# A two-layer fp32 decoder trunk: a seventh-product block more per column group, and weight sums written by adding DMAs

## The chip, the cores and the metric

The kernel runs on one core of a Trainium2 chip, as one launch. The metric is the device time of that launch in microseconds (us). TensorE (PE) multiplies, VectorE (DVE) and ScalarE (ACT) work elementwise, GpSimd (POOL) does small operations, and SyncE (SP) issues the DMAs. In this program POOL's queue can issue DMAs as well.

## The reference

x has 256 tokens of 2048 features; there are two layers, all in fp32. Cut to what matters:

```python
for i in range(2):
    sh1, sc1, g1, sh2, sc2, g2 = split(silu(c) @ w_mod[i] + b_mod[i], 6)
    h = rms_norm(x, norm1_g[i]) * (1 + sc1) + sh1
    y = retention_mixer(h) if i == 0 else short_conv_mixer(h)
    x = x + g1 * y
    h = rms_norm(x, norm2_g[i]) * (1 + sc2) + sh2
    a, b = split(h @ ffn_w_in[i], 2)          # 2048 x 11264
    x = x + g2 * ((silu(a) * b) @ ffn_w_out[i])   # 5632 x 2048
return rms_norm(x, final_g)
```

The feed-forward part (SwiGLU) of each layer multiplies by `ffn_w_in` (first matrix) and `ffn_w_out` (second matrix). They are most of the work.

## The kernel before

**Stages.** The profile shows them one after the other: retention (to about 790 us), the feed-forward of layer 0 ("FFN", to about 1480), the convolution layer (to about 1860) and the feed-forward of layer 1 (the "last stage").

**fp32 by three products.** Every weight tile is split into a rounded part `hi` (ACT, L415) and a remainder `lo` (DVE, L418: raw minus hi); activations are split in the same way. A product is then hi·hi + hi·lo + lo·hi: three matmuls (`thrice`, L481 to L483).

**Weights.** The host lays all weights out in order of use in `w_all`, in chunks of 128 x 2048. SP loads a chunk into one of four buffers `raw` (L376). `prepare` makes pieces of up to 128 x 1024 from it: `hi`, `lo`, and an entry in `ready`. `hi` and `lo` hold five such places, so preparation runs at most five pieces ahead of PE. The same `raw` buffers also take the columns of `w_mod`, each reduced against silu(c) by one DVE instruction over 2048 columns (L322, a "modulation"); there are 160 of these, and `paced` hands them out by a table of due times, `plan_mod`, in units of 128x128 weight tiles used.

**Column groups.** The first matrix of a feed-forward is done in 10 groups after some first columns. A group covers four tiles of `a` and four of `b` (two blocks of 512 columns) and runs through eight pairs of rows ("rows 0 to 7"), each one chunk. It accumulates over the rows in four PSUM banks (`ours`, 128 tokens x 512 each). There are eight banks in all.

**Sevens.** A row given in `IN_SEVEN`, `FFN_SEVEN` or `OUT_SEVEN` is a `Seven`: its 2 x 2 blocks of tokens, rows and columns are multiplied in seven products instead of eight (Strassen's scheme in Winograd's form). That is 7 x 3 matmuls of 512 columns instead of 8 x 3. For the activations, sums of blocks are made once per stage (`made_in_sums`). For the weights, four sums are made per chunk: T1 and T3 in one DVE instruction of 1024 columns (L402, into the tile `differences`), T2 (L406) and T4 (L408) in one of 512 each. The sevens' four extra sums (`p1`, `p5`, `p6`, `p7`) build up in four further banks, and after the group's last seven `mixed_sums` takes them out: one ACT copy (L1202) and four DVE instructions (L1203 to L1206). The next group's `ours` use these banks. After the last row, DVE adds `ours` (L1258), then silu and product follow (L1262, L1263). At row 2 of the next group (`TURNS_AT`, `FFN_TURNS`), PE transposes the result into two banks (`turned`, L1272), and ACT (L1276) and DVE (L1277) split it. The sevens of the next group need those two banks for p1 and p6.

**Order.** Only PE's order (and DVE's and ACT's at the very start) is written by hand. On the other engines a scheduler places the instructions; modulations get a low priority.

Of the kernel before, what the change touches and what calls it, by code (L numbers as in the profile page):

```python
# [260 lines left out]
def trunk(ctx: ExitStack, tc: tile.TileContext, x_in, c_in, pos_in, w_mod, cols_in, gain_in, tab_in, w_all, out):  # L261
# [40 lines left out]
    nc.vector.memset(half, -0.5)  # L302

    flat = [v.rearrange("p a b -> p (a b)") for v in x4]
    differences = [None]


    mod_a = [[const.tile([P, KT], F32, tag=f"a{l}{i}", name=f"a{l}{i}") for i in range(2)] for l in range(DEPTH)]
# [80 lines left out]
    def prepare(between=None):  # L389
        if prepared[0] == len(pieces):  # L390
            return
        index, piece = pieces[prepared[0]]
        prepared[0] += 1
        if piece in (0, 2, 6):
            raws[:] = [next_raw(index)]
            while first <= units[0] < early and len(fetched) < RAW_BUFS - 1 and n_fetched[0] < w_all.shape[0]:
                fetch()
        whole = raws[0]
        b = [whole[:, i : i + DV] for i in range(0, CHUNK, DV)]
        raw = whole[:, :HALF] if piece in (0, 4) else whole[:, HALF:] if piece < 6 else whole  # L400
        if piece == 2:
            nc.vector.tensor_tensor(differences[0], whole[:, DV : 3 * DV], whole[:, : 2 * DV], op=ALU.subtract)  # L402
        elif piece == 3:
            raw = differences[0]
        elif piece == 4:
            nc.vector.tensor_tensor(b[1], b[2], differences[0][:, :DV], op=ALU.subtract)  # L406
        elif piece == 5:
            nc.vector.tensor_tensor(b[3], b[3], b[1], op=ALU.subtract)  # L408
            raw = b[3]
        width, at = raw.shape[1], HALF * (taken_places[0] % PLACES)  # L410
        taken_places[0] += -(-width // HALF)
        hi, lo = [t[:, at : at + width] for t in split_weights]
        steps = [slice(i, min(i + HALF, width)) for i in range(0, width, HALF)]
        for o in steps:
            nc.scalar.copy(hi[:, o], raw[:, o])  # L415
        if between:
            between()
        nc.vector.tensor_tensor(lo, raw, hi.bitcast(F32), op=ALU.subtract)  # L418
        ready.extend((hi[:, o], lo[:, o], o.stop - o.start) for o in steps)

    taken_places = [0]
    split_weights = [
        wpool.tile([P, PLACES * HALF], F32R, tag=tag, name=tag) for tag in ("hi", "lo")
# [34 lines left out]
    def product(g, act, base=0, before=None, banks=None, last=True):  # L458

        fresh = not banks  # L460
        banks = banks or [bank() for _ in g.cols]
        for k in g.ks:
            if before:
                before(k)
            h = act[k - base]
            for c, pt in zip(g.cols, banks):
                hi, lo = take(g, k, c)
                nc.tensor.matmul(  # L468
                    pt, hi, h, start=fresh and k == g.ks[0], stop=False, skip_group_check=True
                )  # L470
                nc.tensor.matmul(  # L471
                    pt[:, 1, :], lo, h[:, 0, :], start=False, stop=last and k == g.ks[-1], skip_group_check=True
                )
            ticked(len(g.cols))
        paced(len(g.cols) * len(g.ks))
        return banks

    def thrice(o, x, w, first, last):
# [14 lines left out]
    def packed(g, act, base=0, before=None, between=None, banks=None, plain=()):  # L493
# [5 lines left out]
        for k in g.ks:  # L499
# [32 lines left out]
                nc.tensor.matmul(pt, lo, h[:, 0, :], start=False, stop=last, skip_group_check=True)  # L532
                at += 1
            ticked(g.n)
        paced(g.n * len(g.ks))
        return banks

    def summed(pt, dst=None, at=slice(0, S)):
# [11 lines left out]

    def squares(acc, t, tag="acc"):
        if acc is None:
            acc = tmp(tag, bufs=1)
            nc.scalar.activation(acc, t, AF.Square)
        else:
            sq = tmp("sq", bufs=2)
# [83 lines left out]
    def normed(accs, layer, norm, g):  # L640
# [18 lines left out]
        for k in g.ks:  # L659
            high, low = raw_all[:, k, : ENDS + S], raw_all[:, k, ENDS + S :]  # L660
            for c, pt in zip(g.cols, banks):
                hi, lo = take(g, k, c)
                nc.tensor.matmul(pt, hi, high, start=k == 0, stop=False, skip_group_check=True)  # L663
                nc.tensor.matmul(pt[:, 2:], hi, low, start=False, stop=False, skip_group_check=True)  # L664
                nc.tensor.matmul(pt, lo, high, start=False, stop=k == KT - 1, skip_group_check=True)  # L665
            if k == ROOTS_AT:
                r = norm_roots(norm_sums(accs), D)
            elif k == SPREAD_AT:
                root = tmp("rb", bufs=1)
                nc.scalar.copy(root, norm_spread(r))  # L670
            elif k > SPREAD_AT:
                more(min(k, made[0] + 2))
        more(KT)
        paced(len(g.cols) * len(g.ks))

        def total(pt, dst=None):
            low_end = tmp("end", (P, 1), bufs=4)
# [478 lines left out]
    def tokens_sums_of(a11, a21, a12, a22, third, others):  # L1156

        u = half_bank()
        s1, s2, s4, s3 = [u[:, n * P : (n + 1) * P] for n in range(4)]
        nc.vector.tensor_tensor(s3, a11, a21, op=ALU.subtract)  # L1160
        nc.vector.tensor_tensor(s1, a21, a22, op=ALU.add)
        nc.vector.tensor_tensor(s2, s1, a11, op=ALU.subtract)
        nc.vector.tensor_tensor(s4, a12, s2, op=ALU.subtract)
# [33 lines left out]
    def mixed_sums(banks):  # L1197

        p1, p5, p6, p7 = banks
        u1, u3 = own["extra"]  # L1200
        u2, u4 = half_bank(), half_bank()
        nc.scalar.copy(u1, p1)  # L1202
        nc.vector.tensor_tensor(u2, p6, u1, op=ALU.add)  # L1203
        nc.vector.tensor_tensor(u3, p7, u2, op=ALU.add)
        nc.vector.tensor_tensor(u4, p5, u3, op=ALU.add)
        nc.vector.tensor_tensor(u2, p5, u2, op=ALU.add)  # L1206
        return {(0, 0): u1, (1, 0): u3, (1, 1): u4, (0, 1): u2}


# [73 lines left out]
    def first_rows(firsts, pairs, layer, norm, turns=()):  # L1283

        pending, done = [], 0
        for i, g in enumerate(firsts):
            pending += [sums(g)] if i else normed(acc, layer, norm, g)
            while len(pending) >= 2:
                both = half_bank().rearrange("p (a b) -> p a b", a=2)
                g1, m = both[:, 0, :], both[:, 1, :]  # L1290
                silu_times(*pending[:2], g1, m)
                pending = pending[2:]
                split(pairs[done // 2][:, done % 2], m)
                done += 1
            for turn_of in turns[4 * (i - 1) : 4 * i] if i else ():
                turn_of()

    def paired(pool, n):
# [3 lines left out]
    with tc.tile_pool(name="ffn", bufs=1) as fpool:  # L1302
        h = rows_at(EARLIER)
        own.update(pool=fpool, sums={}, turns=FFN_TURNS)
        first_mid = paired(fpool, max(FFN_TILES))[: FFN_TILES[0] // 2]
        differences[0] = fpool.tile([P, 2 * DV], F32, tag="differences", name="differences")
        own["extra"] = [fpool.tile([P, DV], F32, tag=f"extra{i}", name=f"extra{i}") for i in range(2)]
        for part in range(2):
            n = FFN_TILES[part] // 2
            mid = paired(fpool, FFN_TILES[part]) if part else first_mid  # L1310
            if not part:
                first_rows(FFN_FIRSTS, mid[-2:], 0, 1)
                made_in_sums(FFN_SEVEN, [
                    fpool.tile([P, 2, P], F32R, tag=f"sums{i}", name=f"sums{i}") for i in range(3 * len(FFN_SEVEN))
                ])
# [48 lines left out]
    differences[0] = flat[2]  # L1364
    xt = [mpool.tile([P, D], F32, tag=f"xt{t}", name=f"xt{t}") for t in range(2)]

    def turn(t, c):
# [15 lines left out]
    def three(v):  # L1383
        return [v[0][:, :, n * P : (n + 1) * P] for n in range(3)] if len(v) == 1 else v

    turns = [lambda t=t, c=c: turn(t, c) for c in range(4) for t in range(2)]


    gate_of = [at(flat[c // 2], c % 2) for c in range(4)]
# [91 lines left out]
    for part in range(2):  # L1481
        n = LAST_TILES[part] // 2
        mid = mids(LAST_TILES[part]) if part else first_mid
        if not part:
            first_rows(LAST_FIRSTS, mid[-2:], 1, 1, turns)
            tmp("beside_sums", (P, BESIDE_SUMS), bufs=1)
            for tag, bufs in (("u", 3), ("low", 2), ("sum", 4)):
# [46 lines left out]
```

## Time and profile before

| what | value |
|---|---|
| median of 3 runs | 2574.0 us (2573.86 to 2575.99) |
| the profiled execution's own time | 2574.43 us |
| its span in the profile | 2572.7 us |
| PE / DVE / ACT / POOL busy | 99% / 89% / 51% / 8% |
| DMA queue of SP, share of 16 engines | 71.5% |
| mean granted TensorE clock | 0.998 |

The span is what the profile shows of the execution; 1.7 us of its own time lie around it. A busy PE is not PE at its peak: its matmuls overlap, so work on PE is counted below by the distance from one start to the next.

### The profile page before, as it was taken

The numbers are of one execution on the slowest core, as the hardware profiler recorded it, in microseconds if no ns is written. First come the engines' busy times: TensorE is split into PE (matmuls) and PEld (weight loads), VectorE is DVE, ScalarE is ACT, GpSimd is POOL, SyncE is SP. The second block draws the span as 40 slices with busy tenths as digits, with TensorE's granted clock in tenths as the row PEclk, the third lists the DMA queues.
The fourth block names the chain that finished last, engine by engine and source line by source line (L and its number), as shares of the span: only waits on it lengthen the run. The fifth ranks groups of instructions, "written<-read, shape, count | busy, mean of one in ns | idle before, by whom it ended". The sixth has DMA issues, their size and how long they took to land.

```text
span 2572.7 us, 35163 instructions
## 1 busy us (share of the span) xinstructions
PE 2553.4 (99%) x13561; PEld 2202.8 (86%) x13561; DVE 2287.4 (89%) x2840; ACT 1312.1 (51%) x1723; POOL 198.8 (8%) x232
## 2 busy tenths in 40 slices
PE   8999999999999999999999999999999999999998
PEld 6898889888889888888888898888998888888887
DVE  7988978888699999888999989988989998899987
ACT  5544543444456554345555454444565554555554
POOL 0000102211000111100001112000000000000002
PEclk9999999999999999999999999999999999999999
DMA  9986769877786777876767869887945565555653
GB/s 399 389 330 234 298 247 351 305 264 296 263 305 235 284 279 289 326 285 249 268 246 288 320 248 351 314 325 271 332 167 214 179 235 206 178 215 183 227 196 131
DMA packets 96697, 689.51 MB, mean 268 GB/s; under 512 B 10744, under 2 KB 12168, under 8 KB 13456
## 3 DMA queue, kind: packets, MB, share of 16 engines
q1 hardware_dynamic: 96528, 687.25, 71.5%
q8 instruction: 106, 1.74, 0.3%
q14 instruction: 63, 0.52, 0.1%
HBM read 685.11 MB, written 2.11 MB: 267 GB/s over the span
## 4 chain that ended last, share of the span: by engine, by line
PE 94%; DVE 3%; DMA 2%; issue 1%; ACT 1%; SPq 0%; ACTq 0%; POOLq 0%; POOL 0%; DVEq 0%
PE bank L481 18%; PE bank L483 18%; PE bank L482 18%; PE bank L468 18%; PE bank L471 10%; PE bank L532 2%; PE bank L531 2%; PE bank L530 2%; PE bank L663 1%; PE bank L665 1%; PE bank L664 1%; DVE lo L418 1%; DMA raw<-w_all 1%; DVE raw L794 1%; PE bank L1272 1%
## 5 line engine op out<-in xcount | busy, mean ns | idle before, releaser
L415 ACT CAST hi<-raw 128x1024 fp32r<-128x1024 f32 (+1 forms) x968 | 983.6, 1025 | 1019.0 <-PE bank L483 459.0
L418 DVE TENSOR_TENSOR lo<-raw,hi 128x1024 fp32r<-128x1024 f32 (+1 forms) x968 | 1134.9, 1185 | 210.6 <-ACT hi L415 204.6
L481 PE MATMUL bank<-hi,h 128*128 128x512 f32 x1580 | 618.3, 391 | 0.0
L483 PE MATMUL bank<-hi,h 128*128 128x512 f32 x1580 | 615.9, 390 | 0.0
L482 PE MATMUL bank<-lo,h 128*128 128x512 f32 x1580 | 615.9, 390 | 0.0
L322 DVE SCALAR_TENSOR_TENSOR raw<-raw,cb 128x2048 f32<-128x2048 f32 x160 | 365.2, 2283 | 8.8 <-DMA raw<-w_mod 8.5
L483 PEld LDWEIGHTS bank<-hi,h 128*128 128x128 f32 x1580 | 296.6, 188 | 62.9
L481 PEld LDWEIGHTS bank<-hi,h 128*128 128x128 f32 x1580 | 296.9, 188 | 59.4
L482 PEld LDWEIGHTS bank<-lo,h 128*128 128x128 f32 x1580 | 296.9, 188 | 59.2 <-DVE lo L418 0.4
L468 PE MATMUL bank<-mid,hi 128*128 128x512 f32 x920 | 319.4, 390 | 0.0
L471 PE MATMUL bank<-mid,lo 128*128 128x256 f32 x920 | 259.4, 282 | 0.0
L468 PE MATMUL bank<-h,hi 128*128 128x512 f32 x736 | 255.4, 390 | 0.0
L471 PE MATMUL bank<-h,lo 128*128 128x256 f32 x736 | 207.4, 282 | 0.0
L468 PEld LDWEIGHTS bank<-mid,hi 128*128 128x128 f32 x920 | 172.6, 188 | 36.2
L471 PEld LDWEIGHTS bank<-mid,lo 128*128 128x128 f32 x920 | 173.9, 189 | 0.1
L468 PE MATMUL bank<-rm,hi 128*128 128x512 f32 x496 | 172.6, 391 | 0.0
L468 PEld LDWEIGHTS bank<-h,hi 128*128 128x128 f32 x736 | 138.1, 188 | 28.9
L532 PE MATMUL bank<-h,lo 128*128 128x256 f32 x488 | 138.5, 284 | 2.6 <-DVE lo L418 2.6
L471 PE MATMUL bank<-rm,lo 128*128 128x256 f32 x496 | 140.1, 282 | 0.2 <-DVE lo L418 0.2
L530 PE MATMUL bank<-h,hi 128*128 128x256 f32 x488 | 138.4, 284 | 1.3 <-ACT h L822 1.3
L471 PEld LDWEIGHTS bank<-h,lo 128*128 128x128 f32 x736 | 139.1, 189 | 0.0
L531 PE MATMUL bank<-h,hi 128*128 128x256 f32 x488 | 138.1, 283 | 0.1
(281 smaller groups left out, 3513.0 us busy)
## 6 DMA issues: line engine op xcount, KB each, us to landing
raw<-w_all SPq DMA_DIRECT2D x456, 1024.0 KB, 4.9
raw<-w_mod SPq DMA_DIRECT2D x192, 1024.0 KB, 5.6
x<-x_in SPq DMA_DIRECT2D x4, 512.0 KB, 5.4
out<-xt SPq DMA_DIRECT2D x4, 512.0 KB, 3.0
decay<-tab_in SPq DMA_DIRECT2D x8, 128.0 KB, 4.7
x<-gate_row SPq DMA_DIRECT2D x2, 512.0 KB, 4.4
last_gain<-gain_in SPq DMA_DIRECT2D x1, 1024.0 KB
cols<-cols_in SPq DMA_DIRECT2D x1, 152.0 KB, 8.1
```

Source lines behind the costliest of these rows:

```text
L322: nc.vector.scalar_tensor_tensor(raw, raw, 1.0, cb, op0=ALU.mult, op1=ALU.mult, accum_out=total)
L415: nc.scalar.copy(hi[:, o], raw[:, o])
L418: nc.vector.tensor_tensor(lo, raw, hi.bitcast(F32), op=ALU.subtract)
L468: nc.tensor.matmul(pt, hi, h, start=fresh and k == g.ks[0], stop=False, skip_group_check=True)
L471: nc.tensor.matmul(pt[:, 1, :], lo, h[:, 0, :], start=False, stop=last and k == g.ks[-1], skip_group_check=True)
L481: nc.tensor.matmul(o, hi, w_hi, start=first, stop=False)
L482: nc.tensor.matmul(o, hi, w_lo, start=False, stop=False)
L483: nc.tensor.matmul(o, lo, w_hi, start=False, stop=last)
L530: nc.tensor.matmul(pt, hi, h[:, 0, :], start=first, stop=False, skip_group_check=True)
L531: nc.tensor.matmul(pt, hi, h[:, 1, :], start=False, stop=False, skip_group_check=True)
L532: nc.tensor.matmul(pt, lo, h[:, 0, :], start=False, stop=last, skip_group_check=True)
L663: nc.tensor.matmul(pt, hi, high, start=k == 0, stop=False, skip_group_check=True)
```

## The change

It makes these edits:

1. `IN_SEVEN` goes from three rows to four of eight (2, 3, 5, 6), and `FFN_SEVEN` from two (3, 5) to three (2, 4, 6).
2. In the last stage T1 and T3 of a seven are no longer made by DVE. SP loads columns 512 to 1535 of the chunk a second time into a sum tile (`sum_begun`), and two prepared pieces later a DMA issued by POOL adds columns 0 to 1023 to it as it writes (`sums_added`). Four sum tiles take turns: the tile `squares_of`, the two halves of a `raw` buffer that is kept from the ring (so three are left for the chunks), and `flat[2]`.
3. All weight sums are now additions; the signs move to the sums of the activations and to `mixed_sums`. In layer 0 DVE still makes T1 and T3.
4. `plan_mod` hands out more modulations in retention and fewer in the FFN, and `paced` is called once per row instead of once per group.
5. Tiles of the norm move into `squares_of`, the order of the transposes of x changes, and the scratch for DMA descriptors is doubled.

```diff
-IN_SEVEN, OUT_SEVEN, TURNS_AT, BESIDE_CB, BESIDE_SUMS = (3, 4, 6), ((2, 4, 6), (2, 4, 6)), 2, 40, 48
+IN_SEVEN, OUT_SEVEN, TURNS_AT, BESIDE_CB, BESIDE_SUMS = (2, 3, 5, 6), ((2, 4, 6), (2, 4, 6)), 2, 40, 48
-FFN_TILES, FFN_SEVEN, FFN_TURNS = (20, 24), (3, 5), 2
+FFN_TILES, FFN_SEVEN, FFN_TURNS = (20, 24), (2, 4, 6), 2
+ADD_AFTER = 2
...
-    plan_mod = [(early, 0), (1024, 22), (1984, 58), (2688, 74), (3008, 88), (3776, 104), (5184, n_mod)]
+    plan_mod = [(early, 0), (1024, 28), (1984, 72), (2688, 84), (3008, 96), (3776, 106), (5184, n_mod)]
...
-        allowed[0] = min(allowed[0] + n * MOST, 2.0) if n <= 64 else 0.0
+        allowed[0] = min(allowed[0] + n * MOST, 2.0)
...
-        if piece == 2:
-            nc.vector.tensor_tensor(differences[0], whole[:, DV : 3 * DV], whole[:, : 2 * DV], op=ALU.subtract)
+        if piece == 2 and index not in summing:
+            summing[index] = sum_tiles[0]
+            nc.vector.tensor_tensor(summing[index], whole[:, DV : 3 * DV], whole[:, : 2 * DV], op=ALU.add)
         elif piece == 3:
-            raw = differences[0]
+            raw = summing[index]
         elif piece == 4:
-            nc.vector.tensor_tensor(b[1], b[2], differences[0][:, :DV], op=ALU.subtract)
+            nc.vector.tensor_tensor(b[1], b[0], summing.pop(index)[:, DV:], op=ALU.add)
         elif piece == 5:
-            nc.vector.tensor_tensor(b[3], b[3], b[1], op=ALU.subtract)
+            nc.vector.tensor_tensor(b[3], b[3], b[1], op=ALU.add)
...
+        if piece == 4:
+            sum_begun()
+        sums_added(1)
+
+    def sum_begun():
+        if len(sums_due) > sums_end[0]:
+            index = sums_due.pop(0)
+            sum_tiles.append(sum_tiles.pop(0))
+            summing[index] = sum_tiles[-1]
+            nc.sync.dma_start(summing[index], w_all[index, :, DV : 3 * DV])
+            adding.append([index, ADD_AFTER])
+
+    def sums_added(n):
+        for a in adding:
+            a[1] -= n
+        while adding and adding[0][1] <= 0:
+            index = adding.pop(0)[0]
+            nc.gpsimd.dma_start(summing[index], w_all[index, :, : 2 * DV], accum_op=ALU.add)
+
+    def sums_from(tiles, end, n):
+        sum_tiles[:], sums_end[0] = tiles, end
+        for _ in range(n):
+            sum_begun()
...
+            if turns and i < 2:
+                tiles = [flat[2], *sum_tiles] if i else [squares_of, *more_sums()]
+                sums_from(tiles, 0, 1 if i else len(tiles))
...
+    def more_sums():
+        held_raw = wpool.tile([P, CHUNK], F32, tag="raw", name=name("raw"), bufs=RAW_BUFS)
+        return [held_raw[:, i : i + 2 * DV] for i in range(0, 4 * DV, 2 * DV)]
```

Three places where the instructions stand differently:

**DVE, end of a column group in the FFN.** `u` and `extra` are the tiles of `mixed_sums` and of the group's end, `lo` the remainders of the weights. Before, from `mixed_sums` (L1203) to the adds of `ours` (L1258):

```order
L1203 TENSOR_TENSOR u_1162_10040<-bank_9936,extra_6782 128x512
L418 TENSOR_TENSOR lo<-raw_10047,hi 128x1024
L1204 TENSOR_TENSOR extra_6783<-bank_9937,u_1162_10040 128x512
L418 TENSOR_TENSOR lo<-raw_10047,hi 128x1024
L1205 TENSOR_TENSOR u_1163_10041<-bank_9935,extra_6783 128x512
L1206 TENSOR_TENSOR u_1162_10040<-bank_9935,u_1162_10040 128x512
L418 TENSOR_TENSOR lo<-raw_10082,hi 128x1024 x2
L1258 TENSOR_TENSOR extra_6782<-bank_9820,extra_6782 128x512
```

With the change the same instructions are L1232 to L1235, L421 and L1287:

```order
L1232 TENSOR_TENSOR u_1166_10133<-bank_9965,extra_6855 128x512
L421 TENSOR_TENSOR lo<-raw_10118,hi 128x1024
L1233 TENSOR_TENSOR extra_6856<-bank_9966,u_1166_10133 128x512
L421 TENSOR_TENSOR lo<-raw_10140,hi 128x1024
L1234 TENSOR_TENSOR u_1167_10134<-bank_9964,extra_6856 128x512
L1235 TENSOR_TENSOR u_1166_10133<-bank_9964,u_1166_10133 128x512
L421 TENSOR_TENSOR lo<-raw_10140,hi 128x1024
L1287 TENSOR_TENSOR extra_6855<-bank_9879,extra_6855 128x512
```

The group's last seven is row 6 instead of row 5, so `mixed_sums` stands one row later: one `lo` lies between it and the adds, where two lay.

**PE, row 2 of a column group in the FFN.** The last of the eight transposes and what follows. Before, row 2 is an ordinary row and goes into the four banks of `ours`:

```order
L1272 MATMUL bank_8067<-tab,extra_6783 128x128
L481 MATMUL bank_7995<-hi,h 128x512
L482 MATMUL bank_7995<-lo,h 128x512
L483 MATMUL bank_7995<-hi,h 128x512
L481 MATMUL bank_7997<-hi,h 128x512
L482 MATMUL bank_7997<-lo,h 128x512
```

With the change it is a seven (`u` are sums of activations):

```order
L1301 MATMUL bank_8163<-tab,extra_6856 128x128
L508 MATMUL bank_8085<-hi,u_7441 128x512
L509 MATMUL bank_8085<-lo,u_7441 128x512
L510 MATMUL bank_8085<-hi,u_7441 128x512
L508 MATMUL bank_8084<-hi,h 128x512
L509 MATMUL bank_8084<-lo,h 128x512
L510 MATMUL bank_8084<-hi,h 128x512
L508 MATMUL bank_8171<-hi,u_7443 128x512
```

The seven begins right behind the transposes; its fifth product (p1) needs the first of the two banks that the transposes just wrote, its sixth (p6) the second. In the last stage rows 2 and 3 stand in the same way.

**SP, steady part of the last stage.** Loads of chunks (`raw` from `w_all`, 128x2048). Before, there is nothing else in its queue:

```order
L376 DMA raw_2085_18993<-w_all 128x2048
L376 DMA raw_2086_19011<-w_all 128x2048
L376 DMA raw_2089_19033<-w_all 128x2048
L376 DMA raw_2094_19075<-w_all 128x2048
L376 DMA raw_2095_19105<-w_all 128x2048
```

With the change (128x1024 are the first halves of the sums):

```order
L378 DMA raw_2065_19293<-w_all 128x2048
L432 DMA raw_1836_16436<-w_all 128x1024
L378 DMA raw_2066_19311<-w_all 128x2048
L432 DMA x8_75<-w_all 128x1024
L378 DMA raw_2067_19358<-w_all 128x2048
L378 DMA raw_2068_19393<-w_all 128x2048
L432 DMA squares_81<-w_all 128x1024
L378 DMA raw_2069_19411<-w_all 128x2048
L432 DMA raw_1836_16436<-w_all 128x1024
L378 DMA raw_2072_19433<-w_all 128x2048
```

Of eight chunks of a group four are followed by a load into a sum tile (`squares`, the two halves of raw_1836, `x8`, which is `flat[2]`). Each waits until DVE has read its tile for the last time (T2 of a seven whose chunk stands two loads further up), and fills it for the seven four further on.

More of the change, by code (lines that the diff above doesn't have):

```diff
@@ L304, in trunk @@
     flat = [v.rearrange("p a b -> p (a b)") for v in x4]
-    differences = [None]
+    squares_of = const.tile([P, 4 * S], F32, tag="squares", name="squares")
+    n_squares = [0]
     mod_a = [[const.tile([P, KT], F32, tag=f"a{l}{i}", name=f"a{l}{i}") for i in range(2)] for l in range(DEPTH)]
@@ L419, in prepare @@
         ready.extend((hi[:, o], lo[:, o], o.stop - o.start) for o in steps)
+        if piece == 4:
[18 more added lines that the diff above has]
+            sum_begun()
+    summing, sums_due, sum_tiles, sums_end, adding = {}, [], [], [0], []
     taken_places = [0]
@@ L474, in product @@
             ticked(len(g.cols))
-        paced(len(g.cols) * len(g.ks))
+            paced(len(g.cols))
         return banks
@@ L672, in normed @@
                 more(min(k, made[0] + 2))
+            paced(len(g.cols))
         more(KT)
-        paced(len(g.cols) * len(g.ks))
         def total(pt, dst=None):
@@ L1305, in trunk @@
         first_mid = paired(fpool, max(FFN_TILES))[: FFN_TILES[0] // 2]
-        differences[0] = fpool.tile([P, 2 * DV], F32, tag="differences", name="differences")
+        sum_tiles[:] = [fpool.tile([P, 2 * DV], F32, tag="weights", name="weights")]
+        last_sevens = sum(isinstance(g, Seven) for part in range(2) for g in sum(LAST_IN[part] + LAST_OUT[part], []))
+        sums_due[:], sums_end[0] = sorted(in_seven)[-last_sevens:], last_sevens
         own["extra"] = [fpool.tile([P, DV], F32, tag=f"extra{i}", name=f"extra{i}") for i in range(2)]
@@ L1313, in trunk @@
                 made_in_sums(FFN_SEVEN, [
-                    fpool.tile([P, 2, P], F32R, tag=f"sums{i}", name=f"sums{i}") for i in range(3 * len(FFN_SEVEN))
-                ])
+                    fpool.tile([P, 2, P], F32R, tag=f"sums{i}", name=f"sums{i}") for i in range(6)
+                ] + [tmp("u", (P, 2, P), F32R, bufs=3) for _ in range(3)])
             for i, groups in enumerate(FFN_IN[part]):
@@ L1384, in three @@
         return [v[0][:, :, n * P : (n + 1) * P] for n in range(3)] if len(v) == 1 else v
-    turns = [lambda t=t, c=c: turn(t, c) for c in range(4) for t in range(2)]
+    turns = [lambda t=t, c=c: turn(t, c) for c in (2, 3, 0, 1) for t in range(2)]
     gate_of = [at(flat[c // 2], c % 2) for c in range(4)]
@@ L1486, in trunk @@
             tmp("beside_sums", (P, BESIDE_SUMS), bufs=1)
-            for tag, bufs in (("u", 3), ("low", 2), ("sum", 4)):
+            for tag, bufs in (("u", 3), ("low", 2), ("sum", 4), ("rb", 1)):
                 single_sums.extend(tmp(tag, (P, 2, P), F32R, bufs=bufs) for _ in range(bufs))
```

21 lines of the change are left out of this document (11 added, 10 removed).

## The prediction

> **What bounds the kernel now.** I read the page first, then the waits of PE, then each stage in the table of windows.
>
> ```profile
> span 2572.7 us, 35163 instructions
> PE 2553.4 (99%) x13561; PEld 2202.8 (86%) x13561; DVE 2287.4 (89%) x2840; ACT 1312.1 (51%) x1723; POOL 198.8 (8%) x232
> ...
> PE bank L589 <- POOL rs L921: 3.5, 1, 3.5
> PE bank L532 <- DVE lo L418: 2.6, 3, 1.4
> ...
> PE bank L471 <- DVE lo L418: 0.2, 1, 0.2
> ```
>
> The last three rows are PE's waits: who waited for whom, total us, times, longest. Nothing after the start is above 0.2 us. So time can only be won by taking work from PE, and at most what is taken.
>
> The next rows are windows from one group's transposes to the next group's: length, then PE, PEld, DVE, ACT and POOL busy, clock, DMA share, GB/s. The first four are FFN groups (two sevens), the last two are in the last stage (three sevens).
>
> ```profile
> 875.49:918.79 43.30, 43.30 (x195) 35.74 (x194) 42.55 (x47) 22.43 (x25) 8.49 (x8) 1.00 0.79 291
> 918.79:962.10 43.31, 43.31 (x196) 35.74 (x194) 40.68 (x47) 22.44 (x25) 8.11 (x6) 1.00 0.74 268
> 1159.65:1202.97 43.32, 43.32 (x195) 35.75 (x194) 39.59 (x44) 22.40 (x25) 1.29 (x2) 1.00 0.66 242
> 1202.97:1246.28 43.31, 43.31 (x195) 35.75 (x194) 40.58 (x45) 22.54 (x25) 3.32 (x3) 1.00 0.72 267
> ...
> 2277.05:2319.45 42.40, 42.40 (x193) 35.18 (x191) 39.85 (x50) 25.18 (x30) 0.00 (x0) 1.00 0.55 200
> 2319.45:2361.85 42.40, 42.40 (x193) 35.17 (x191) 39.85 (x50) 25.18 (x30) 0.00 (x0) 1.00 0.54 198
> ```
>
> PE fills every window; DVE has 0.75 to 3.7 us left in an FFN group and 2.55 in the last stage. DVE is the engine that could take over.
>
> **Removed from PE.** A matmul's "busy" overlaps the next one, so I take the distance of starts. Thirty matmuls in a row, first and last (start, duration):
>
> ```profile
> 2005.08 0.40 PE L481 MATMUL bank<-hi,h 128*128 128x512 f32 x1
> ...
> 2011.66 0.39 PE L483 MATMUL bank<-hi,h 128*128 128x512 f32 x1
> ```
>
> (2011.66 - 2005.08) / 29 = 0.227 us. One more seven saves three matmuls in each of the ten groups of the FFN and the ten of the last stage: 20 x 3 x 0.227 = 13.6 us, 6.8 in each. All of it lies on PE's chain. An FFN group shrinks to 43.31 - 0.68 = 42.63, a group of the last stage to 41.72. (The FFN's and the last stage's groups already differ by one seven, and by 0.91 us; the 0.23 above 0.68 I don't count on.)
>
> **Added to DVE, per seven.** Starts of DVE's instructions in an FFN group:
>
> ```profile
> 1241.05 1.22 DVE L402 TENSOR_TENSOR differences<-raw 128x1024 f32<-128x1024 f32 x1
> 1242.18 1.22 DVE L418 TENSOR_TENSOR lo<-raw,hi 128x1024 fp32r<-128x1024 f32 x1
> 1243.32 0.69 DVE L406 TENSOR_TENSOR raw<-raw,differences 128x512 f32<-128x512 f32 x1
> 1243.92 2.29 DVE L322 SCALAR_TENSOR_TENSOR raw<-raw,cb 128x2048 f32<-128x2048 f32 x1
> 1246.13 0.08 DVE L322 DVE_READ_ACCUMULATOR raw<-raw,cb 128x1 f32 x1
> ```
>
> So 1.14 us for 1024 columns, 0.60 for 512, 2.21 for a modulation. An ordinary row costs two `lo` (2.28). A seven costs the sum, three `lo`, T2, T4 and a `lo` of 512: 4 x 1.14 + 3 x 0.60 = 6.36, so 4.08 more; without the sum, 2.94 more.
>
> *FFN.* In the DVE order the groups 2 to 4 lose 1.3 modulations each (10 to 6 in three), 5 to 10 lose 1.2 (16 to 9 in six). Groups 2 to 4: (42.55 + 40.68) / 2 + 4.08 - 1.3 x 2.21 = 42.8 of 42.63; groups 5 to 10: 40.1 + 4.08 - 1.2 x 2.21 = 41.5 of 42.63. DVE is at its limit in the first, just below it in the second.
>
> The first group is worse. In its columns and rows DVE had one idle moment at 800 and the next at 863:
>
> ```profile
> 800.32 0.48 DVE L607 SCALAR_TENSOR_TENSOR h<-u,s,h 128x256 fp32r<-128x256 f32 x1 [0.38 <-PE bank L665]
> 863.17 1.23 DVE L418 TENSOR_TENSOR lo<-raw,hi 128x1024 fp32r<-128x1024 f32 x1 [0.19 <-ACT hi L415]
> ```
>
> 63 us without a gap. The change puts a seven into it (4.08) and the sums of activations for it (about 2.4, an estimate from 2 instructions of 256 and 8 of 128 columns at the same rate), with as many modulations as before: DVE ends 6.5 us late, PE 0.68 early. Earlier that would have been covered. These rows show by how much, FFN first, then the last stage (last of `mixed_sums`, first add of `ours`):
>
> ```profile
> 1272.23 0.68 DVE L1206 TENSOR_TENSOR u<-bank,u 128x512 f32<-128x512 f32 x1
> ...
> 1279.04 0.68 DVE L1258 TENSOR_TENSOR extra<-bank,extra 128x512 f32<-128x512 f32 x1
> ...
> 2032.71 0.68 DVE L1206 TENSOR_TENSOR u<-bank,u 128x512 f32<-128x512 f32 x1
> 2034.44 0.68 DVE L1258 TENSOR_TENSOR x<-bank,x 128x512 f32<-128x512 f32 x1
> ```
>
> The next group's fourth accumulator needs the bank that L1206 frees, nine matmuls (2.0 us) into the group, and the adds start when the group ends. With the last seven in row 5, L1206 ended 6.1 us before that; in row 6, as the last stage has it, 1.05. Cover shrinks from about 8 us to about 3. So of 6.5 + 0.7 us lateness about 4.2 reach PE at the start of group 2 (bounds 0, if DVE works off the delay, and 7.2). For the other nine FFN groups I take 1.3 in all (0 to 9 x 1.0).
>
> The second deadline: PE's transposes, then DVE's split of them.
>
> ```profile
> 1246.28 1.03 PE L1272 MATMUL bank<-tab,extra 128*128 128x128 f32 x8
> 1247.07 0.48 PE L481 MATMUL bank<-hi,h 128*128 128x512 f32 x1
> ...
> 1248.75 1.28 DVE L1277 TENSOR_TENSOR mid<-bank,mid 128x512 fp32r<-128x512 f32 x2
> ```
>
> PE goes on at 1247.07 (0.79 later); with a seven in row 2, p1 needs the first bank 12 matmuls on, at 1249.79, p6 the second at 1250.47. DVE would be done at about 1249.4 and 1250.03. It just fits when DVE is on time, so I cost it at nothing; if DVE is late, it costs the lateness, inside the term above.
>
> *Last stage.* One seven more, four sums fewer to make: 2.94 - 3 x 1.14 = -0.48 per group, 39.4 of 41.72. DVE is no closer to its limit. What is new are DMAs. A group moves 8 chunks of 1.05 MB in 42.4 us (200 GB/s at a share of 0.55). Now four loads and four adds of 0.52 MB come on top: 12.6 MB in 41.72 us, 302 GB/s, if an add costs what a load costs. No row shows an adding DMA. Below, it can't be cheaper than the load it contains; above, if reading and writing back count double, the load is like 352 GB/s, at three times 402. The fastest that this profile shows, and what one chunk takes to land:
>
> ```profile
> GB/s 399 389 330 234 298 247 351 305 264 296 263 305 235 284 279 289 326 285 249 268 246 288 320 248 351 314 325 271 332 167 214 179 235 206 178 215 183 227 196 131
> ...
> raw<-w_all SPq DMA_DIRECT2D x456, 1024.0 KB, 4.9
> ```
>
> I take twice: it fits. Latency of the sums is covered: a tile is filled for the seven four further on, some 42 us. SP's new waits stand behind loads that are ready earlier, so they delay the chunk after them little. The ring loses one of four buffers: a chunk comes due every 5.2 us and must land in 5 to 8, with 3 in flight. I take 1 us in all (0 to 5).
>
> *Retention and convolution.* 13 modulations (28.7 us of DVE) move in front of 790 us. PE there:
>
> ```profile
> 385.00:740.00 355.00, 355.00 (x2030) 313.55 (x2029) 294.57 (x356) 158.72 (x209) 48.74 (x58) 1.00 0.78 292
> ```
>
> 60 us of DVE idle take them; 1 us for bad moments (0 to 4). ACT gains 1.6 us per seven at 52%: hidden. Signs and moved tiles: same instructions, nothing.
>
> **Sum.** 13.6 - 4.2 - 1.3 - 1 - 1 = 6.1 us. Against the profiled execution's own 2574.43 this gives 2568.3; the median, 2574.0, is 0.4 below that run, so 2568.
>
> **POOL and DVE.** One row says that POOL can be shut out:
>
> ```profile
> 2513.60 10.46 POOL L1428 TENSOR_TENSOR sums<-total 128x1 f32<-128x1 f32 x1 [648.83 <-ACT u L1478]
> ```
>
> An operation on one column took 10.46 us while DVE ran two-input instructions without a gap. The Trainium skill, page "SBUF — State Buffer", section "Who interferes with whom", states that a DVE instruction with two SBUF inputs contends with a GpSimd instruction that reads SBUF, and infers that writing DMA descriptors doesn't need that side. By the first half the row is explained; by the second the adds would cost nothing here, and the sum stays as it is. Its warning that DMAs issued by POOL starve would hold only if DVE ran its two-port modes. No run here shows descriptors being made.
>
> **The rivals.**
>
> *A: DVE becomes the bound in every FFN group (0.15).* DVE's idle time now (2.7 to 3.7 us of 43.31 in groups 5 to 10) is of the kind of the row at 863.17, waiting for ACT, and may stay. Then a group lasts 41.5 + 2.9 = 44.4 instead of 42.63; ten groups lose 18 us, and 4 in the first: 2574 - 13.6 + 18 + 4 + 2 = 2584. Against it: the idle moments come when DVE is ahead, and go when it falls behind.
>
> *B: adding DMAs take the engines (0.10).* It decides from three times a load's price, 402 GB/s. At four times, (8.4 + 2.1 + 8.4) MB at 400 GB/s are 47.2 us per group, 5.5 too many in ten: 2574 - 13.6 + 55 + 5 = 2620. For it: no price known. Against: the share of 0.55 leaves room.
>
> *C: making the descriptors shares DVE's port (0.12).* If each add stops DVE for as long as a common POOL operation (median 1.1 us, row below), four per group are 4.4 against 2.3 of slack: 2.1 x 10 = 21 us, 2574 - 13.6 + 21 + 5 = 2586. If instead POOL is stopped, 10.46 us each just fit, four in 41.7.
>
> ```profile
> L332 POOL TENSOR_TENSOR g<-msum,cols x64: 189/1104/1110, 220.5 to 1861.3; 128x1 f32<-128x1 f32 x64
> ```
>
> *D: three buffers are too few (0.08).* The chunk loads arrive late and the last stage gives back its 6.8: 2574 - 13.6 + 6.8 + 6.5 = 2574, no change.
>
> **How the numbers follow.** Forecast 0.55, rivals 0.45. 0.2% is 5.1 us, about what a measurement can tell from no change. The forecast lies one us beyond that; with its terms at their bounds it reaches from 2560.4 to about 2578. I give 0.40 of it to faster and 0.15 to same. A: 0.03 same, 0.12 slower. B: slower. C: 0.02 same, 0.10 slower. D: 0.02 faster, 0.02 same, 0.04 slower. Faster 0.42, same 0.22, slower 0.36. The range goes from the full 13.6 (2560) to 2590; outside lie B and the worse part of C.
>
> **What would show it.** PE's waits: some 4 us at the first matmuls of the second FFN group, on L1232 to L1235; hardly any in the last stage. Windows: 42.6 and 41.7 us per group, DVE over 41 in the FFN and 39.4 in the last stage, DMA share there 0.8 to 0.95. Wrong: waits of PE on `lo` throughout a stage (A), ACT waiting for the sum tiles' DMA (B), DVE's `lo` longer than 1.22 (C), or ACT's `hi` waiting for `raw` (D).

## The result, and the profile after

The changed kernel takes 2595.8 us (median of four runs, 2594.9 to 2604.3) against 2574.0 us: a ratio of 1.0091, 95% interval 1.0079 to 1.0103. It is 22 us slower; 2568 us and a gain were forecast. The profiled execution took 2596.17 us. From its page, the span and the engines:

```profile
span 2594.4 us, 35412 instructions
PE 2554.6 (98%) x13501; PEld 2193.6 (85%) x13501; DVE 2306.9 (89%) x2908; ACT 1342.1 (52%) x1771; POOL 217.6 (8%) x284
```

PE has 60 matmuls less and a longer span. The transposes of a group (L1272 before, L1301 after) are good marks for where the time went: their first and last start stand behind the durations, the FFN's in the first row, the last stage's in the second. Before:

```profile
L1272 PE MATMUL bank<-tab,extra x80: 270/272/273, 875.5 to 1371.6; 128*128 128x128 f32 x80
L1272 PE MATMUL bank<-tab,x x80: 270/272/273, 1959.7 to 2447.4; 128*128 128x128 f32 x80
```

After:

```profile
L1301 PE MATMUL bank<-tab,extra x80: 270/272/330, 875.7 to 1367.2; 128*128 128x128 f32 x80
L1301 PE MATMUL bank<-tab,x x80: 270/272/328, 1959.5 to 2468.5; 128*128 128x128 f32 x80
```

Retention: +0.2 us. FFN: 491.5 instead of 496.1, -4.6. From there to the first mark of the last stage: 592.3 instead of 588.1, +4.2. Last stage: 509.0 instead of 487.7, **+21.3**. After it: 125.9 instead of 125.3, +0.6. The sum is +21.7, the difference of the spans. Windows from one group's transposes to the next group's, as in the prediction (length, PE, PEld, DVE, ACT, POOL busy, clock, DMA share, GB/s); the first three are FFN groups, the others lie in the last stage:

```profile
875.66:919.62 43.96, 42.95 (x192) 35.09 (x191) 43.36 (x49) 24.66 (x28) 4.35 (x4) 1.00 0.65 240
919.62:962.25 42.63, 42.63 (x192) 35.17 (x191) 42.18 (x48) 24.18 (x27) 4.38 (x3) 1.00 0.67 246
1201.28:1243.92 42.64, 42.64 (x192) 35.17 (x191) 40.60 (x46) 24.10 (x27) 1.10 (x1) 1.00 0.61 222
1959.53:2006.60 47.07, 44.07 (x189) 35.63 (x188) 40.60 (x48) 26.47 (x31) 3.53 (x4) 0.96 0.87 279
2006.60:2048.47 41.87, 41.87 (x190) 34.52 (x188) 35.38 (x45) 24.64 (x30) 3.52 (x4) 1.00 0.91 289
2048.47:2099.09 50.62, 45.85 (x190) 36.57 (x189) 43.69 (x56) 28.09 (x35) 3.54 (x4) 0.93 0.82 269
2417.54:2467.77 50.23, 44.21 (x189) 35.55 (x188) 43.22 (x52) 26.68 (x32) 3.52 (x4) 0.97 0.87 287
```

The FFN does what was forecast, 42.63 us per group. The last stage has a DMA share of 0.82 to 0.91 instead of 0.55; some groups run at 41.9 us, three of the shown ones lose 5 to 9 us, at a granted clock below 1. PE's four largest waits, over the whole run (total us, times, longest):

```profile
PE bank L508 <- DVE u L1235: 7.7, 6, 2.4
PE bank L508 <- DVE mid L1306: 5.9, 4, 2.8
PE bank L618 <- POOL rs L950: 3.5, 1, 3.5
PE bank L508 <- ACT row L1436: 2.8, 1, 2.8
```

L618 stood there before (as L589). L1235 and L1306 are the two deadlines of the prediction, the banks of `mixed_sums` and the split of the transposes; of their 13.6 us 12.2 lie in the last stage. L1436 is a small ACT copy in the last stage; it stands right behind a `hi` (ACT, 2087.26) that waited 3.00 us for its chunk. With 0.9 us behind the product at a group's end (L1292), PE waits 15.9 us in the last stage. PE's row names only the last link. The link ahead of it is seen from the side of the DMA: who waited for the chunk loads of the last stage (line, us, times), and how long they took to land. Before (L376):

```profile
  DVE x L402: 0.4, 1
DMA to landing us min/median/max: 4.7/4.8/6.3
```

After (L378):

```profile
  ACT hi L418: 78.0, 32
  DVE raw L409: 17.7, 11
DMA to landing us min/median/max: 4.8/7.6/12.7
```

And the adding DMAs of the last stage (L440). The list of those who waited for them is empty:

```profile
who waited for it (us, times):
busy tenths in 40 slices 0000000000000000000000000000000000000000
DMA to landing us min/median/max: 6.3/10.0/13.1
```

So the sums arrive in time; it is the chunks themselves that come late. One such chain, ACT first (two late chunks), then PE:

```profile
2038.64 2.01 ACT L418 CAST hi<-raw 128x1024 fp32r<-128x1024 f32 x2 [4.71 <-DMA raw<-w_all]
2043.68 1.05 ACT L418 CAST hi<-raw 128x1024 fp32r<-128x1024 f32 x1 [3.04 <-DMA raw<-w_all]
```

```profile
2051.90 0.39 PE L510 MATMUL bank<-hi,h 128*128 128x512 f32 x1
2054.27 0.50 PE L508 MATMUL bank<-hi,h 128*128 128x512 f32 x1 [1.99 <-DVE mid L1306]
...
2056.72 0.63 PE L508 MATMUL bank<-hi,h 128*128 128x512 f32 x1
2057.14 0.63 PE L509 MATMUL bank<-lo,h 128*128 128x512 f32 x1
```

ACT is kept 7.8 us by two chunks, DVE, which needs ACT's `hi`, falls behind with it, and some 10 us later PE waits for the split before row 2's seven. After the wait its matmuls stand 0.42 to 0.43 us apart instead of 0.227, for some 3 us.

### The profile page after: what moved, and what is told of

The parts are those of the page before. It is cut to its first block, busy times and chain, and to the rows that moved or that the text cites. A ratio compares the mean times of both kernels' runs of the same rounds, so it can differ in the third digit from the quotient of the medians.

```text
span 2594.4 us, 35412 instructions
## 1 busy us (share of the span) xinstructions
PE 2554.6 (98%) x13501; PEld 2193.6 (85%) x13501; DVE 2306.9 (89%) x2908; ACT 1342.1 (52%) x1771; POOL 217.6 (8%) x284
## 5 line engine op out<-in xcount | busy, mean ns | idle before, releaser
L418 ACT CAST hi<-raw 128x1024 fp32r<-128x1024 f32 (+1 forms) x1014 | 1019.6, 1018 | 1029.0 <-PE bank L510 336.0
L421 DVE TENSOR_TENSOR lo<-raw,hi 128x1024 fp32r<-128x1024 f32 (+1 forms) x1014 | 1173.4, 1175 | 181.1 <-ACT hi L418 177.7
L508 PE MATMUL bank<-hi,h 128*128 128x512 f32 x1500 | 588.4, 392 | 12.0 <-DVE mid L1306 5.9
L509 PE MATMUL bank<-lo,h 128*128 128x512 f32 x1500 | 586.4, 391 | 1.9 <-DVE lo L421 1.8
L510 PE MATMUL bank<-hi,h 128*128 128x512 f32 x1500 | 586.1, 391 | 0.0
L508 PEld LDWEIGHTS bank<-hi,h 128*128 128x128 f32 x1500 | 282.2, 188 | 74.2 <-DVE u L1235 7.9
L509 PEld LDWEIGHTS bank<-lo,h 128*128 128x128 f32 x1500 | 282.4, 188 | 60.8 <-DVE lo L421 4.0
L510 PEld LDWEIGHTS bank<-hi,h 128*128 128x128 f32 x1500 | 282.2, 188 | 60.1
```

The lines of the kernel that those rows point to most:

```text
L508: nc.tensor.matmul(o, hi, w_hi, start=first, stop=False)
L509: nc.tensor.matmul(o, hi, w_lo, start=False, stop=False)
L510: nc.tensor.matmul(o, lo, w_hi, start=False, stop=last)
```

## Experiments

Theories at the start: **Q**, SP's queue (the load of a sum tile waits for its tile, chunk loads stand behind it); **B**, the adding DMAs take too much of the DMA engines; **D**, three buffers are too few. Ratios are to before, with their 95% interval. The edits are cut to their main lines.

**1. The FFN's part alone, and three buffers alone.**

```diff
-IN_SEVEN = (2, 3, 5, 6)
+IN_SEVEN = (3, 4, 6)
 # ffn_only, in the last stage: sums by DVE into flat[2], nothing held
-tiles = [flat[2], *sum_tiles] if i else [squares_of, *more_sums()]
-sums_from(tiles, 0, 1 if i else len(tiles))
+sum_tiles[:] = [flat[2]]
 # three_buffers: instead, by DVE into the held buffer
+if not i: sum_tiles[:] = more_sums()[:1]
```

> The changed kernel, but its last stage as before: sevens in rows 3, 4, 6, all four weight sums made by DVE, four buffers for the chunks, no second loads and no adding DMAs. Three theories for the changed kernel's loss, which its trace puts between 1900 us and the end: Q, SP's queue: the load of a sum tile waits for its tile and the chunk loads stand behind it; B, the adding DMAs cost the DMA engines too much; D, three buffers are too few. All three expect the same here: the FFN keeps what it gained up to its last group (1366.48 against 1370.89 us, and 0.68 still to come: 5.1 us), so 2574.0 - 5.1 = 2569 us, and no wait of PE above 1 us after 960 us. If the FFN's part is itself paid for later, by modulations moved behind it, it is 2574 and the waits lie in the convolution.

> As the run before (last stage with sevens 3, 4, 6, sums by DVE, no second loads), but the chunks of the last stage have three buffers, the fourth being kept for DVE's sums. D: the loads land late, ACT's hi waits for raw by tens of us and the time is 2575 to 2595 us. Q and B: a chunk still lands in about 5 us at 200 GB/s with two loads in flight, so it stays within 2 us of the run before, about 2569 us.

Measured: 2571.3 us (ratio 0.9986, 0.9977 to 0.9996) and 2571.2 us (0.9989, 0.9979 to 0.9998). Three buffers by themselves cost nothing: D alone falls. The FFN's part is worth 2.7 us, not 5.1:

```profile
L1301 PE MATMUL bank<-tab,extra x80: 270/272/328, 875.4 to 1367.0; 128*128 128x128 f32 x80
L1301 PE MATMUL bank<-tab,x x80: 270/272/273, 1956.3 to 2444.0; 128*128 128x128 f32 x80
```

Of the 4.5 us gained up to 1367.0, 1.2 are given back before the last stage begins (589.3 us between the marks instead of 588.1), though the last group's own 0.7 falls into this stretch. PE's waits there sum to 0.9 us. But in three_buffers, of the same median time, this stretch takes 588.1 us and the first mark stands at 878.4 instead of 875.4: profiled executions differ by up to 3 us in stretches where nothing was changed. Where the missing 2.4 us go stays open.

**2. The DMAs taken away in three steps.**

```diff
 # no_sum_dmas: tiles set to zero once, neither load nor add
-nc.sync.dma_start(summing[index], w_all[index, :, DV : 3 * DV])
-adding.append([index, ADD_AFTER])
 # no_adds: the loads stay
-nc.gpsimd.dma_start(summing[index], w_all[index, :, : 2 * DV], accum_op=ALU.add)
 # plain_adds: the same bytes, overwriting
-nc.gpsimd.dma_start(summing[index], w_all[index, :, : 2 * DV], accum_op=ALU.add)
+nc.gpsimd.dma_start(summing[index], w_all[index, :, : 2 * DV])
```

> The changed kernel without the second loads and without the adding DMAs: the four sum tiles are set to zero once, so the products with T1 and T3 come out wrong, and T2 and T4 too; all instructions of PE, ACT and DVE, the four sevens and the three buffers stay. D: the loss stays, 2590 us or more. Q and B: the last stage runs at 41.7 us per group, and the time is 2569 - 6.8 = 2562 us.

The second of the three ran later than the other two, with theory **BD** (adds lengthen each chunk's landing, and only a ring of three can't take that), which run 1 and the other two had suggested:

> The changed kernel with the second loads on SP but without POOL's adding DMAs (T1 and T3 come out as the loaded columns alone). Q: SP waits for the tiles as before, and the loss stays: over 2585 us. B and BD: each DMA's share of the engines counts; half the plain case's extra bytes cost half of its loss or less (2576.1 - 2566.3 = 9.8 us): 2567 to 2571 us.

> The changed kernel with POOL's DMAs as plain loads of the same bytes that overwrite the tile and don't add: T1 and T3 come out wrong, every wait, queue and byte stays. If an adding DMA holds the engines for twice a load's time (5.6% of the span for 27.27 MB against 73.5% for 714.52 MB), 52 of them give back 2.8% of the span in engine time. B: the DMA share in the last stage's groups falls from 0.9 to about 0.78 and most of the loss goes: 2565 to 2575 us. Q and D: SP's waits are the same, so at most a third of it goes: 2587 to 2594 us.

Measured: 2566.3, 2568.9 and 2576.1 us (in the order of the list above); with adds 2595.8. These three leave out the sums, or half of each, and only their times count. D alone falls again, no_adds lies where BD put it, and plain_adds 1 us above what B allowed. Landing of a chunk in the last stage without sum DMAs, with loads, and with plain second loads, one row of each run:

```profile
DMA to landing us min/median/max: 4.6/4.8/7.4
```

```profile
DMA to landing us min/median/max: 4.6/5.3/8.7
```

```profile
DMA to landing us min/median/max: 4.6/7.2/10.3
```

Time and landing go up together, 7.4 to 12.7 us at the longest, and ACT's waits for chunks with them (9.5, 37.2, 45.8, 78.0 us). Between the marks the last stage takes 482.5, 484.9, 495.2 and 509.0 us: with three buffers throughout, the sum DMAs cost it 26.5 us. Without them it runs as forecast, DVE included:

```profile
1998.70:2040.54 41.84, 41.84 (x189) 34.50 (x188) 39.16 (x50) 26.60 (x32) 0.00 (x0) 1.00 0.54 201
```

The price of an add, from the DMA queues of the last stage (packets, MB, share of 16 engines over 490 us), with adds and with plain loads in their place:

```profile
q1 hardware_dynamic: 19111, 115.94, 63.8%
q0 software_dynamic: 5839, 21.30, 23.2%
```

```profile
q0 software_dynamic: 6048, 22.02, 13.1%
```

Per MB: 0.550% on SP's queue, 1.089% for an add, 0.595% for the plain load from POOL. An add costs 1.98 times a load on SP's queue: the value that was taken. SP still waits for the sum tiles in no_adds, and that run loses 2.6 us; so Q by itself is not the cause.

**3. A fourth buffer, with two sum tiles instead of four.**

```diff
-tiles = [flat[2], *sum_tiles] if i else [squares_of, *more_sums()]
+tiles = [flat[2], *sum_tiles] if i else [squares_of]
```

> The changed kernel with four buffers for the chunks in the last stage and two sum tiles (squares_of and flat[2]) instead of four; loads, adds and sevens stay. So far: without the second loads and adds 2566.3 us, with plain loads instead of adds 2576.1, as changed 2595.8; three buffers alone cost nothing (2571.2 with and without). Theory BD: the sum DMAs lengthen each chunk's landing (4.9 to about 9 us in the last stage) and only together with a ring of three does this stall ACT; a fourth buffer gives one more transfer in flight (10.4 us of cover instead of 5.2), so 2570 to 2580 us with the DMA share still near 0.9. Theory B: at a share of 0.9 the engines are simply full, and the time stays at 2590 to 2600. Theory T: with two tiles, half the cover, the sums come late themselves (ACT's hi of a sum tile waits for POOL's DMA): 2600 us or more.

Measured: 2625.6 us (1.0200, 1.0183 to 1.0218). The time is theory T's, not BD's 2570 to 2580, and the trace shows the exchange. Who waited for the chunks:

```profile
  ACT hi L418: 6.1, 2
  DVE raw L409: 5.8, 3
DMA to landing us min/median/max: 4.7/7.2/11.0
```

And for the adds:

```profile
  DVE raw L409: 68.6, 14
  ACT hi L418: 13.9, 4
```

The chunks take as long to land as in the changed kernel (median 7.2), and with a fourth buffer hardly anybody waits for them: 12 us instead of 96. The waits have moved to the sums, whose tiles now have half the time. This does not isolate the ring: sums that come late hold the preparation back, and that alone gives the chunks more time. Four sum tiles and four buffers together were not run.

**4. Two buffers, no sum DMA at all.**

```diff
 # against three_buffers; the two tiles take turns
-sum_tiles[:] = more_sums()[:1]
+sum_tiles[:] = [more_sums()[0], more_sums()[0]]
```

> The run with three buffers and DVE's sums (2571.2 us), with one buffer less: two for the chunks of the last stage, no second loads, no adds, sevens in rows 3, 4, 6. It asks whether the time between a buffer's release and its next landing is what the changed kernel lacks. Three buffers give 3 x 5.3 = 15.9 us per turn, of which a transfer of 9 to 12 us, as in the changed kernel's last stage, leaves 4 to 7 for the conversion; two give 10.6, of which one of 4.8 us leaves 5.8. Theory R, ring and landing: the same squeeze without any sum DMA, ACT's hi waits for raw by 50 us or more, 2580 to 2610 us. If not R, that is if the loss hangs on the adds themselves (their writes, their tiles): within 4 us of 2571.

Measured: 2590.5 us (1.0064, 1.0048 to 1.0081), 19 us over three buffers. Who waited for the chunks:

```profile
  ACT hi L419: 149.3, 53
  DVE raw L406: 25.4, 14
DMA to landing us min/median/max: 4.7/4.8/8.9
```

Here the transfer is short and the ring is short; in the changed kernel the ring has three and the transfer is long. Both make ACT wait for chunks and lose 19 and 26 us; three buffers with short transfers do neither (run 1). The last link differs: with two buffers PE's weight loads wait for `lo` (22.3 us in 39 waits) and the clock stays at 1.00. So a ring that is too short for its transfers is enough for a loss of this order: a buffer's turn, from its release over SP's queue and the landing to the end of the conversion, has to fit into as many rows as there are buffers. That the changed kernel's loss needs the ring of three is argued from this and from run 3, not shown.

**5. SP's queue.** The second loads issued by POOL, so that no chunk load stands behind a sum tile:

```diff
-nc.sync.dma_start(summing[index], w_all[index, :, DV : 3 * DV])
+nc.gpsimd.dma_start(summing[index], w_all[index, :, DV : 3 * DV])
```

> The changed kernel with the second loads issued by POOL too, in front of the adds, so that nothing in SP's queue waits for a sum tile. Q: SP's waits at these loads (159 us in the last stage) kept the chunk loads back; without them the time falls to 2570 to 2580 us. B and BD: after such a wait the next chunk load waited for its own buffer in any case, so the time stays within 6 us of 2595.8.

Measured: 2586.1 us (1.0046, 1.0031 to 1.0061), 9.7 less than as changed: more than B allowed, less than Q. Who waited for the chunks, and their landing:

```profile
  ACT hi L418: 46.5, 28
  DVE raw L409: 25.8, 14
DMA to landing us min/median/max: 4.7/7.3/11.7
```

The last stage takes 496.1 us between the marks instead of 509.0: half of its 26.5 us goes, and the waits for chunks fall from 96 to 72 us, while a chunk lands 0.3 us earlier (median). So the median landing alone does not give the size of the loss. The second loads' place in SP's queue may have a share in it; but plain_adds, with SP's queue as changed, gives back as much (495.2), and here the adds, too, land earlier than as changed (7.7 us in the median instead of 10.0). The run does not divide the loss between the queue's order and the landing.

**6. Fewer sums by DMA, or none.** Rows 2 and 5 by DVE, rows 3 and 6 by DMA; the same with the loads on POOL (the edit of 5); and all four by DVE:

```diff
 # half_by_dve
-if piece == 4: sum_begun()
+if piece == 4 and index in by_dma: sum_begun()
...
-sums_due[:] = sorted(in_seven)[-last_sevens:]
+sums_due[:] = sorted(in_seven)[-last_sevens:][1::2]
 # four_sevens_by_dve
-sums_from(tiles, 0, 1 if i else len(tiles))
+sum_tiles[:] = [flat[2]]
```

> The changed kernel with two of the four sevens of a group (rows 2 and 5) summed by DVE into a held tile, and two (rows 3 and 6) by DMA with three rotating tiles; three buffers. The DMA share goes from 0.9 to about 0.72, DVE from 39.4 to 39.4 + 2 x 1.14 = 41.7 us of a group of 41.8. B and BD: the DMA loss shrinks by more than half, to 5 to 10 us over 2566.3, plus what DVE at its limit costs (0 to 10): 2570 to 2585 us. Q: half the waits, half the loss: about 2581. If DVE is the bound instead, PE waits for lo and mid with no wait of ACT for DMA.

> The run half_by_dve (2580.6 us: two sevens of a group summed by DVE, two by DMAs) with the second loads issued by POOL in front of the adds, so that SP's queue holds nothing but chunk loads. With four sevens by DMA this was worth 9.7 us, so with half as many 5: 2576 us. It can't be under the 2566.3 of the run without sums plus what DVE at its limit (41.7 of 41.8 us) costs; if it is under 2571 it is the best version so far.

> The changed kernel with its four sevens of eight rows in the last stage, but all weight sums made by DVE into one tile, no second loads, no adds, four buffers. DVE then has 39.4 + 4 x 1.14 = 44.0 us to do in a group that PE does in 41.8: ten groups x 2.2 = 22 us over the 2566.3 us without sums, 2588 us; if DVE's short idle moments (2.4 us per group) stay, 2610. If DVE makes up for it between the groups' ends, no less than 2580. It tells what the adding DMAs were worth against the way without them.

Measured: 2580.6 us (1.0030, 1.0018 to 1.0042; single runs 2574.5 to 2590.4), 2587.0 us (1.0044, 1.0029 to 1.0059) and 2582.6 us (1.0033, 1.0020 to 1.0046). The first fits BD and Q alike. The second missed: with half the sums, moving the loads to POOL gained nothing, so run 5's 9.7 us is no fixed price of SP's queue. A group of the last one:

```profile
2003.60:2046.92 43.32, 42.12 (x189) 34.49 (x188) 42.76 (x54) 26.62 (x32) 0.00 (x0) 1.00 0.51 194
```

DVE is the bound there, 42.76 busy in 43.32 us. So the adding DMAs were worth less than nothing: the same sevens with DVE's sums are 13 us faster than with theirs, and three sevens by DVE (2571.3) are the best of all.

**7. Refills moved into the ordinary rows.**

```diff
-if piece == 4: sum_begun()
+if piece == 1 and len(summing) < len(sum_tiles): sum_begun(hi)
+# in sum_begun, ahead of the load:
+nc.scalar.copy(summing[index][:, :1], after[:, :1].bitcast(F32))
```

> The changed kernel, but the refill of a sum tile no longer begins in the seven that frees it (rows 2, 3, 5, 6); it begins in the ordinary rows 4, 7, 0 and 1, behind an ACT copy of one column of that row's hi into the tile. The same DMAs, buffers, tiles and sevens. Theory L, crowding in place: the sum DMAs all fall into the 25 us of rows 2 to 6, where with five chunks and adds at twice a load's price they need 5.2 + 2.1 + 4.2 = 11.5 MB, 460 GB/s, over the 400 that this kernel ever reaches; spread over six rows and with the tiles long free (no wait of SP in front of chunk loads) this is under 400, and the time falls to 2568 to 2582 us. Theory BD, the average share of 0.9 of a whole group with a ring of three: the bytes per group are the same, so 2588 to 2600 us.

Measured: 2629.3 us (1.0206, 1.0189 to 1.0223); both theories missed it. The landing of the chunks from 2350 to 2410 us of this run:

```profile
DMA to landing us min/median/max: 4.8/7.7/17.8
```

The refills were to be spread and were not: three loads of sum tiles and their three adds were issued between 2379.9 and 2396.4 us, and a chunk load among them landed 17.8 us later. The DMA share from 2380 to 2400 is 0.9 to 1.05, in the five microseconds from 2360 it is 0.03. So theory L was not put to its test; the run shows the longest landing of a chunk where loads and adds of sums crowd together.

## Why the prediction was wrong

- **Removed from PE: right.** 42.63 us per FFN group to the second digit; 41.8 instead of 41.72 in the last stage without sum DMAs. The 13.6 us of matmuls are gone.
- **FFN, start of group 2: right mechanism, too large.** PE waits 1.0 us on L1235 and the group takes 43.96 us, 1.3 lost instead of 4.2; in the others nothing instead of 1.3. Retention cost 0.2 instead of 1 in the profiled execution (14 modulations moved ahead of 790 us, 13 were counted). Not foreseen was a loss between the FFN and the last stage: with the sum DMAs, which begin at 1864 us, this stretch takes 592.3 us against 589.5 in no_sum_dmas, and PE waits 2.8 us in it instead of 1.0; the rest of the difference, and the 1.2 us of ffn_only, are within what executions differ by.
- **Price of an add: right** (1.98 times a load, twice was taken); the DMA share of 0.8 to 0.95 came out at 0.82 to 0.91 in the rows above.
- **"I take twice: it fits": this step failed.** It compared bytes with capacity over a whole group. Under a share of 0.9 the chunks, which go through the same 16 engines, land in 7.6 us (median), up to 12.7, instead of 4.8 (6.3 at most). And **"a chunk must land in 5 to 8 ... I take 1 us in all (0 to 5)"** set the ring against the landing of before. The two were costed apart, each rightly (three buffers cost 0, run 1; the adds' engine time fits on average), and together the last stage pays 26.5 us for them (482.5 us between the marks in no_sum_dmas, 509.0 in the changed kernel) where the sum has 1. **"so they delay the chunk after them little"**, on SP's new waits, belongs to this step: it holds without adds (no_adds, 2.6 us for the second loads and their waits together), and with them the loads' place in the queue may have a share, which the runs don't settle (run 5).
- **DVE in the last stage: right** (39.2 us without sum DMAs). That PE would hardly wait in the last stage fell with the step above: of the 26.5 us its waits are 15.9 and the lower clock after them, by an estimate from the rows below, 6.8 (four times 3.4 us at half); some 4 us are not placed.
- **The covers at L1235 and L1306** were worked out for the FFN and held there, but for the 1.0 us above. In the last stage late chunks used them up: the row "if DVE is late, it costs the lateness" was the one that paid.
- **Rivals.** A did not occur. B needed three times a load's price; at two the engines were not full on average, and the loss came from chunks that landed late. C did not show: DVE's `lo` of 1024 columns took 1.22 us (mean), as before. D had the sign of ACT waiting for `raw`, which is what happened, but its cause (three buffers) needed B's adds, and its price, 6.8 us, was a quarter of the real one. No rival joined the two, so 2596 lay outside the range. The terms at their upper bounds (7.2, 9, 5 and 4) give 2586, not the "about 2578" of the prediction; that too is less than was measured.
- **POOL and DVE.** POOL's issue of an add took 0.88 us (0.88 to 0.90 for the last stage's 42); the sum was right to leave this out.

The version that beats both kernels is the FFN's part alone: 2571.3 us, 0.14% under before (0.04 to 0.23%).

## What to carry to other kernels

A transfer that fits the DMA engines on average can still lengthen the others beside it: here the chunks' median landing went from 4.8 to 7.6 us. Cost an added DMA by what it does to the landing time of those already there, and check that against the ring: buffers times row time, less the conversion and the time a load stands behind others in its queue, is what landing may take. Where a change adds traffic and takes a buffer in the same edit, cost the two as one term.

## What the runs showed of the hardware

- **An adding DMA takes 1.98 times the engine time per byte** of a load on SP's queue (1.83 times a plain load from POOL), and landed in 10.0 us (median) for 0.5 MB.
- **A wait of PE can cost more than its length.** After the wait of 1.99 us at 2054.27 the matmuls stand 0.43 us apart for about 3 us, with a granted clock of 0.68 from 2055 to 2060; after one of 2.76 us at 2425.19 they stand 0.23 us apart at once, and the clock stays at 1.00:

```profile
2055.00:2060.00 5.00, 5.00 (x17) 3.81 (x16) 4.84 (x9) 2.72 (x4) 0.00 (x0) 0.68 0.91 243
2425.20:2430.20 5.00, 5.00 (x22) 4.14 (x23) 5.00 (x6) 3.44 (x4) 0.34 (x1) 1.00 0.93 256
```

  Of the last stage's five longest waits four (1.99, 2.33, 2.37 and 2.78 us) were followed by 3.4 us at a clock of 0.50 or 0.51, and the one of 2.76 was not: the length of a wait alone does not decide. In the shown groups with waits the clock is 0.93 to 0.97, by an estimate worth 1.5 to 3.5 us each. The Trainium skill, page "TensorE: Matmul & The Clock Gate", section "Part 1: The HAM clock gate (the "warmup" mystery)", gives 426.7 ns between matmuls of 512 columns when the array is cold, and says it goes cold after an idle window of about 3.4 us. The distance agrees with the 0.43 us of these rows; the idle time does not, here 1.99 us were enough.
